# Attention's probabilities turned from streamed operand to weights in a one-core encoder block

## The chip, the core and the metric

The kernel runs on one core of a Trainium2 chip. A core has TensorE (PE; its weight loads are shown apart as PEld), VectorE (DVE), ScalarE (ACT), GpSimd (POOL) and a queue for transfers (SP). The metric is the device time of one execution in microseconds (us). The time given is the median of several runs; one more execution was taken by the profiler, and all rows of the trace come from that one.

## What is computed

One layer of an encoder block on 512 tokens of width 1024, in float32: a half step of a gated feed-forward net, then two token mixers side by side (an RWKV-7 recurrence and a "forgetting" attention, each 8 heads of 64), a gated sum of both, and a second half step. The change touches the attention:

```
def forgetting_attention(q, k, v, log_f):
    scale = 1.0 / np.sqrt(hd).astype(np.float32)
    cum = jnp.cumsum(log_f, axis=-1)
    ...
        s = jnp.einsum('bhqd,bhkd->bhqk', q_i, k, preferred_element_type=jnp.float32) * scale
        s = s + c_i[..., :, None] - cum[..., None, :]
        s = jnp.where(mask, s, -jnp.inf)
        pr = jax.nn.softmax(s, axis=-1)
        return jnp.einsum('bhqk,bhkd->bhqd', pr.astype(v.dtype), v)
```

The mask is causal, and the queries come in 4 blocks of 128. Query block b sees b + 1 blocks of 128 keys.

## The kernel before

Activations lie transposed, features on the partitions and the 512 tokens along the free dimension. Products that need near-float32 accuracy are made of three one-pass products of parts (`mm3`, L142). The attention's product with the values and the scan's small products take float32 operands as they are, and each such matmul shows as two instructions ("passes") in the trace, each with a weight load of its own.

The stage of the change runs two things at once and fills the rest. (a) The recurrence goes through 16 chunks of 32 tokens. Each chunk has three visits of TensorE with narrow weights of 32 or 64 columns: `product_x` (xps), `product_u` (ups) and `products_sy` (sps, yps). (b) The attention goes through four pairs of heads, and for each pair through three `Block`s: query blocks 0 and 1 together, then 2, then 3. (c) What is left of the input projection, columns pq and pgt of eight steps with three matmuls of 512 columns each, fills TensorE's time ("fills", rank FILL).

One `Block` (L1785) does this for its two heads q = 0, 1. `logits` (L1793): TensorE writes the logits of a head into a PSUM bank `lp` (tile pool pf, three banks). `maximum` (L1805): VectorE masks and takes the row extreme into `mx`. `exp` (L1813): ScalarE writes the exponentials to `pts` and their sum to `mx`. `divide` (L1817): VectorE takes the reciprocal of the sums and multiplies the probabilities by it, one instruction per query block and head. `turn` (L1824): TensorE transposes the probabilities, 128x128 at a time, back into `lp`. `copy_t` (L1828): ScalarE copies them to `tr`. `values` (L1832): the values `vt` are the weights (128 keys x 64), the transposed probabilities are streamed (128 queries), and the result stands transposed already, head q on partitions 64q to 64q + 63 of `lp[1]`. `copy_o` (L1841): VectorE copies it to its place in `qp`.

The order of the stage's instructions isn't left to the order of the code. `Plan` (L177) gets each step with an engine, an estimated duration, its dependencies, a rank (SCAN, SIDE, NEXT, ROWS, FILL) and the buffers that it takes and frees. `start` (L192) gives the earliest time that a step could begin, `run` (L208) makes the list by picking the step that begins first (the longer remaining way wins a tie), and writes the instructions in that order. `SWITCH` holds a price for each change between kinds of TensorE work ("w" 512-column products, "t" transposes, "m", "n" and "u" narrow ones). `Queued` (L60) holds VectorE, ScalarE and TensorE to the written order, and all their instructions of this stage then carry its line, L71. In `enter` (L1844) a block's steps are given to the plan. When the stage ends, the centering products `yc` (`first`, L1924) and the output projections `ppj` follow.

Of the kernel before, what the change touches and what calls it, by code (L numbers as in the profile page):

```python
# [9 lines left out]
F32 = mybir.dt.float32  # L10
# [3 lines left out]
ALU = mybir.AluOpType  # L14
# [4 lines left out]
P = 128  # L19
# [9 lines left out]
NB = T // P  # L29
# [21 lines left out]
def kernel(  # L51
# [24 lines left out]
    dve, act, pe = [Queued(e, False) for e in (nc.vector, nc.scalar, nc.tensor)]  # L76
# [97 lines left out]
    def on(do, *a):  # L174
        return lambda: do(*a)

    class Plan:  # L177
# [9 lines left out]
        def op(s, engine, us, do, *deps, rank=0, takes=(), frees=(), later=0.0, kind="w"):  # L187
            s.ops.append(dict(engine=engine, us=us, do=do, deps=deps, rank=rank, takes=takes, frees=frees, later=later,
                              kind=kind, end=None, way=0.0))
            return s.ops[-1]  # L190

        def start(s, o):  # L192
            to, now = o["engine"], s.idle.get(o["engine"], 0.0)
            ahead = 0.0 if to != "PE" else 0.57 if o["rank"] == SCAN else 0.26 if o["rank"] == SIDE and o["kind"] in "tw" else 0.31
            for d in o["deps"]:
                if d["end"] is None:
                    return None
                by = d["engine"]
                lag = 0.32 if by == "PE" else 0.15 if by == to else 0.21
                now = max(now, d["end"] + (0.0 if by == to == "PE" else lag + ahead))  # L200
            for name in set(o["takes"]):
                n = sum(t == name for t in o["takes"])
                if len(s.room[name]) < n:
                    return None
                now = max(now, sorted(s.room[name])[n - 1])
            return now

        def run(s):  # L208
            todo = list(s.ops)
            for o in s.ops[::-1]:  # L210
                o["way"] = o["way"] + o["us"] if o["rank"] != FILL else 0.0
                for d in o["deps"]:
                    d["way"] = max(d["way"], o["way"] + 0.3)
            while todo:
                at = {n: now for n, o in enumerate(todo) for now in [s.start(o)] if now is not None}

                def first(n):
                    o = todo[n]
                    turn = o["engine"] == "PE" and o["kind"] == "t" and s.kind in "mnu"
                    return at[n], -o["way"] - (40.0 if turn else 0.0), n  # L220

                n = min(at, key=first)
                o = todo[n]
                if o["engine"] in ("DVE", "ACT") and o["rank"] != SCAN:
                    until = at[n] + 0.98 * o["us"]
                    n = next((m for m in at if todo[m]["engine"] == o["engine"] and todo[m]["rank"] == SCAN
                              and at[m] < until), n)
                o = todo.pop(n)
                us = o["us"]
                if o["engine"] == "PE":  # L230
                    change = "".join("n" if k in "mnu" else k for k in (s.kind, o["kind"]))
                    us += s.SWITCH.get(change, 0.0) if s.kind != o["kind"] else 0.0
                    s.kind = o["kind"]
                s.idle[o["engine"]] = at[n] + us
                o["end"] = at[n] + us + o["later"]
                for name in o["takes"]:
                    s.room[name].remove(min(s.room[name]))
                for name in o["frees"]:
                    s.room[name].append(o["end"] + 0.33)
                if o["do"]:  # L240
                    o["do"]()

# [15 lines left out]
    class Norm:  # L258
# [7 lines left out]
        def scale(s, c, eng=None, src=None):  # L266
            g = pc(s.gain + c)
            src = xT[c][:] if src is None else src
            hi, lo = pair("h", c, s.place), pair("l", c, s.place)
            if eng is act:  # L270
                high = act.activation(hi[:], src, AF.Copy, scale=g)
            else:
                high = dve.tensor_scalar(hi[:], src, g, None, op0=ALU.mult)
            low = dve.scalar_tensor_tensor(lo[:], src, g, hi[:].bitcast(F32),
                                           op0=ALU.mult, op1=ALU.subtract)
            s.hi[c], s.lo[c] = hi, lo
            return high, low
# [813 lines left out]
    with ExitStack() as mx:  # L1091
# [302 lines left out]
        def half(q):  # L1394
            return slice(q * 64, (q + 1) * 64)

        class Rows(Columns):
# [26 lines left out]
            def sum(s, behind=None):  # L1424
                lo = s.part(1) if s.part else tmp("slo", dt=F32R)
                dve.tensor_tensor(lo[:], s.sq[:], f32(s.hi[:]), op=ALU.subtract)
                s.ps = bank("pq2", pf)
                with tc.issue_after(behind.ins) if behind else ExitStack():
                    for i, part in enumerate((s.hi, lo)):
                        last = pe.matmul(s.ps[:], bonesr[:], part[:], start=i == 0, stop=i == 1)  # L1430
                return last
# [18 lines left out]
        vt = []  # L1450
# [334 lines left out]
        class Block:  # L1785
# [13 lines left out]
                    pe.matmul(l, qb[q][:, bs], klc[q][:, 0:n], start=False, stop=True)  # L1799

            def of(s, q, b):
                mx = s.pair.mx[q]
                return slice(s.at[b], s.at[b] + (b + 1) * P), mx[:, b:b + 1], mx[:, NB + b:NB + b + 1]

            def maximum(s, q, b):  # L1805
                if s.pair.mx is None:
                    s.pair.mx = [tp.tile([P, 2 * NB], F32, tag=f"mx{i}", name=f"mx{i}", bufs=2) for i in range(2)]
                n, top, _ = s.of(q, b)
                l = s.lp[q][:, n]
                dve.tensor_tensor_reduce(l, l, dmask[:, T - (b + 1) * P:T], -1.0, 3e38, op0=ALU.add, op1=ALU.min,  # L1810
                                         accum_out=top)
# [2 lines left out]
                n, top, sum_ = s.of(q, b)  # L1814
                act.activation(pts[:, q, n], s.lp[q][:, n], AF.Exp, bias=top, scale=-1.0, accum_out=sum_)

            def divide(s, q):  # L1817
                sums = s.pair.mx[q][:, NB + s.bl[0]:NB + s.bl[-1] + 1]
                dve.reciprocal(sums, sums)
                for b in s.bl:  # L1820
                    n, _, sum_ = s.of(q, b)
                    dve.tensor_scalar(pts[:, q, n], pts[:, q, n], sum_, None, op0=ALU.mult)

            def turn(s, q):  # L1824
                for k in range(s.w // P):
# [5 lines left out]

            def values(s):  # L1832
                for j, b in enumerate(s.bl):
                    for k in range(b + 1):
                        o = s.at[b] + k * P
                        for q in range(2):
                            h = 2 * s.pair.p + q
                            pe.matmul(s.lp[1][half(q), j * P:(j + 1) * P], vt[k][:, h * 64:(h + 1) * 64],
                                      s.tr[q][:, o:o + P], start=k == 0, stop=k == b)

            def copy_o(s):  # L1841
                dve.tensor_copy(s.pair.qp[:, s.bl[0] * P:(s.bl[-1] + 1) * P], s.lp[1][:, 0:len(s.bl) * P])

            def enter(s, operands):  # L1844
                for q in range(2):
                    us = sum(0.455 * (b + 1) * P / T + 0.02 for b in s.bl)
                    sees.append(op("PE", us, on(s.logits, q), *operands[q], rank=SIDE, takes=["pf"]))
                lit = sees[-2:]
                for q in range(2):
                    o = []  # L1850
                    for b in s.bl:
                        n = (b + 1) * P
                        e = op("DVE", 0.18 + 1.05e-3 * n, on(s.maximum, q, b), lit[q], rank=SIDE)
                        o.append(op("ACT", 0.26 + 0.83e-3 * n, on(s.exp, q, b), e, *turned[q][-1:], rank=SIDE))
                    exps.extend(o)
                    us = 0.16 + sum(0.13 + 0.69e-3 * (b + 1) * P for b in s.bl)
                    o = op("DVE", us, on(s.divide, q), *o, rank=SIDE)
                    lit[q] = op("PE", 0.11 * s.w / P, on(s.turn, q), o, rank=SIDE, kind="t")
                for q in range(2):
                    turned[q].append(lit[q])  # L1860
                o = [op("ACT", 0.1 + 0.75e-3 * s.w, on(s.copy_t, q), lit[q], *copies[-1:], rank=SIDE, takes=["tr"],
                        frees=["pf"] * (1 - q)) for q in range(2)]
                copies.append(o[1])
                us = 0.22 * sum(b + 1 for b in s.bl)
                o = op("PE", us, s.values, *o, rank=SIDE, frees=["tr"] * 2, kind="n")
                return op("DVE", 0.13 + 0.55e-3 * len(s.bl) * P, s.copy_o, o, rank=SIDE, frees=["pf"])

        outs = []
        for p in range(NP):
# [314 lines left out]
```

## Time and profile before

| what | value |
|---|---|
| median of 3 runs | 1098.98 us (1097.88 to 1099.1) |
| the profiled execution | 1097.66 us |
| span of its instructions | 1095.8 us |
| clock granted to TensorE, mean | 0.998 |
| the 80 transposes of probabilities (lp<-ident,pts), busy | 13.0 us |
| the 160 passes of the values (lp<-tr,vt), busy | 11.4 us |

In the rows of a group stand the engine, the operation, what is written and read (for a matmul the streamed operand first, then the weights), the weights' rows*columns and the streamed shape, the count, the busy time, the mean duration of one in ns, and the idle time of the engine ahead of them. In the rows of a timeline stand the start and the duration in us; neighbours of one kind are merged into one row with their count. A matmul's duration holds its way through the array, so successive matmuls overlap, and the distance of their starts tells what one costs.

### The profile page before, as it was taken

To read this page: it belongs to the slowest core of one execution; us is meant where nothing else is said; L and a number is where in the kernel's file an instruction comes from. 1 tells how busy PE (TensorE), PEld (TensorE's weight loads), DVE (VectorE), ACT (ScalarE), POOL (GpSimd) and SP (SyncE) were. 2 spreads that over 40 slices of the span, in tenths; PEclk is the share of its full clock that TensorE was granted. 3 is DMA by queue.
4 is the path that set the end of the run, shared out by engine and by line. 5 is a ranking of instruction groups with operands and counts; after the bars stand their busy time and mean duration, and the time that the engine had idled before them with its cause. 6 is when DMAs were issued, how large, how long until landed. Compare 5 with 4: busy or idle time off the path is not lost.

```text
span 1095.8 us, 16697 instructions
## 1 busy us (share of the span) xinstructions
PE 1087.1 (99%) x6306; PEld 887.4 (81%) x6306; DVE 837.8 (76%) x1162; ACT 670.1 (61%) x1050; POOL 212.5 (19%) x255
## 2 busy tenths in 40 slices
PE   9999999999999999999999999999999999999997
PEld 7888888888887888888777777888888888888886
DVE  7997676789756699788877766877697766689874
ACT  6765556575554755346988856534576565576554
POOL 1211220134204112401000030112311202114210
PEclk9999999999999999999999999999999999999999
DMA  7989887879936434444112252645968888859972
GB/s 225 250 174 235 198 178 202 192 143 191 231 98 184 114 94 128 114 136 116 50 41 84 81 200 88 189 118 172 271 153 192 189 215 174 184 158 203 236 187 77
DMA packets 139725, 177.11 MB, mean 162 GB/s; under 512 B 9726, under 2 KB 75838, under 8 KB 139646
## 3 DMA queue, kind: packets, MB, share of 16 engines
q0 software_dynamic: 33328, 70.40, 33.7%
q1 hardware_dynamic: 105582, 104.21, 31.1%
q10 hardware_dynamic: 736, 1.45, 0.3%
q8 instruction: 50, 0.82, 0.3%
q14 instruction: 29, 0.24, 0.1%
HBM read 163.51 MB, written 12.52 MB: 161 GB/s over the span
## 4 chain that ended last, share of the span: by engine, by line
PE 97%; ACT 2%; DVE 1%; issue 0%; DVEq 0%; ACTq 0%
PE P L71 39%; PE P L145 5%; PE P L144 5%; PE P L143 5%; PE pgt L71 5%; PE lp L71 3%; PE pq L71 2%; PE ppj L71 2%; PE pk L145 2%; PE pk L143 2%; PE pk L144 2%; PE pb L71 2%; PE pa L71 1%; PE pw L144 1%; PE pw L145 1%; PE pw L143 1%
## 5 line engine op out<-in xcount | busy, mean ns | idle before, releaser
L71 PE MATMUL P<-sraw,q 128*128 128x512 f32 x344 | 91.3, 389 | 0.0
L135 ACT CAST whi<-raw 128x1024 fp32r<-128x1024 f32 (+3 forms) x43 | 41.1, 956 | 65.8 <-issue 19.3
L71 PEld LDWEIGHTS P<-sraw,q 128*128 128x128 f32 x344 | 64.6, 188 | 13.4
L71 PE MATMUL P<-swhi,q 128*128 128x512 f32 x224 | 71.4, 390 | 0.0
L71 PE MATMUL P<-sraw,wxh 128*128 128x512 f32 x200 | 68.4, 394 | 0.0
L136 DVE TENSOR_TENSOR wlo<-raw,whi 128x1024 fp32r<-128x1024 f32 (+3 forms) x44 | 49.6, 1127 | 16.3 <-ACT whi L135 15.2
L71 PE MATMUL P<-swhi,wxh 128*128 128x512 f32 x144 | 56.9, 395 | 0.0
L71 PE MATMUL P<-swhi,wxl 128*128 128x512 f32 x144 | 56.1, 390 | 0.0
L71 PE MATMUL P<-swlo,wxh 128*128 128x512 f32 x144 | 56.1, 389 | 0.0
L704 POOL DMA_DIRECT2D cb<-in_ffn_w_dram x20 | 24.1, 1204 | 150.1 <-DVE cd L71 85.3
L71 PE MATMUL P<-sraw,wxl 128*128 128x512 f32 x136 | 53.0, 390 | 0.0
L704 POOL DMA_DIRECT2D cd<-in_ffn_w_dram x24 | 29.5, 1229 | 102.6 <-DVE swlo L71 38.7
L71 PEld LDWEIGHTS P<-swhi,q 128*128 128x128 f32 x224 | 42.0, 188 | 8.7
L71 PE MATMUL P<-swlo,q 128*128 128x512 f32 x112 | 43.6, 389 | 0.0
L71 PEld LDWEIGHTS P<-sraw,wxh 128*128 128x128 f32 x200 | 37.2, 188 | 7.3
L71 ACT CAST sraw<-cd 128x1024 fp32r<-128x1024 f32 x30 | 31.5, 1050 | 15.1 <-PE P L71 11.5
L71 DVE TENSOR_TENSOR swlo<-ca,swhi 128x1024 fp32r<-128x1024 f32 x24 | 29.2, 1222 | 14.0 <-ACT swhi L71 14.0
L71 DVE TENSOR_TENSOR swlo<-cc,swhi 128x1024 fp32r<-128x1024 f32 x20 | 24.5, 1224 | 19.0 <-ACT swhi L71 18.7
L71 DVE TENSOR_TENSOR u<-P,u 128x512 f32<-128x512 f32 x52 | 34.1, 684 | 5.8 <-ACT u L71 5.7
L563 POOL DMA_DIRECT2D ca<-in_ffn_w_dram x16 | 19.3, 1205 | 96.2 <-DVE swlo L71 66.4
L143 PE MATMUL pk<-xh,whi 128*128 128x512 f32 x96 | 37.8, 394 | 0.0
L145 PE MATMUL pk<-xh,wlo 128*128 128x512 f32 x96 | 37.5, 391 | 0.2 <-DVE wlo L136 0.2
(616 smaller groups left out, 3446.9 us busy)
## 6 DMA issues: line engine op xcount, KB each, us to landing
raw<-in_w_in_dram SPq DMA_DIRECT2D x40, 512.0 KB
cc<-in_ffn_w_dram SPq DMA_DIRECT2D x36, 512.0 KB
cb<-in_ffn_w_dram POOLq DMA_DIRECT2D x36, 512.0 KB, 6.1
cb<-in_ffn_w_dram SPq DMA_DIRECT2D x32, 512.0 KB
cd<-in_ffn_w_dram POOLq DMA_DIRECT2D x32, 512.0 KB, 7.5
ca<-in_ffn_w_dram POOLq DMA_DIRECT2D x32, 512.0 KB, 7.6
ca<-in_ffn_w_dram SPq DMA_DIRECT2D x20, 512.0 KB
cd<-in_ffn_w_dram SPq DMA_DIRECT2D x18, 512.0 KB
```

Source lines behind the costliest of these rows:

```text
L71: q.last = do(*a, **kw)
L135: (hi_eng or act).copy(hi[:], raw[:])
L136: (eng or dve).tensor_tensor(lo[:], raw[:], hi[:].bitcast(F32), op=ALU.subtract)
L143: pe.matmul(ps, whi, xhi, start=first, stop=False, skip_group_check=onto)
L144: pe.matmul(ps, whi, xlo, start=False, stop=False, skip_group_check=onto)
L145: return pe.matmul(ps, wlo, xhi, start=False, stop=last, skip_group_check=onto)
L563: nc.gpsimd.dma_start(s.sum[g], src, accum_op=ALU.add)
L704: nc.gpsimd.dma_start(to, s.block(b, n, h), accum_op=ALU.add)
```

## The change

The values' product is turned round. The transposed probabilities become the weights (128 keys x 128 queries) and the values are streamed (64 columns), so the result stands with the queries on the partitions and the two heads side by side, 64 columns each. The probabilities are no longer divided: `divide` takes the reciprocals of the sums of both heads in one instruction (`mx` is now one tile for both), and `scale` multiplies the result by them as it reads it from PSUM, one instruction for a block. `turn_o` then transposes the result on TensorE, 128x128 for each query block, into another part of the same bank, and `copy_o` copies from there. So `turn` no longer waits for `divide`; `turn_o` waits for `scale`.

The plan's constants for delays, ties and switches are others, the values now count as kind "t", and the estimate of the values' duration stays 0.22 us for two heads and one block of keys. The list of the whole stage is made anew with them. Nothing outside the stage is edited, and no transfer is added or removed.

```
@@ -191,12 +191,13 @@
 
         def start(s, o):
             to, now = o["engine"], s.idle.get(o["engine"], 0.0)
-            ahead = 0.0 if to != "PE" else 0.57 if o["rank"] == SCAN else 0.26 if o["rank"] == SIDE and o["kind"] in "tw" else 0.31
+            ahead = 0.0 if to != "PE" else 0.74 if o["rank"] == SCAN else 0.29 if o["rank"] == SIDE else 0.3
+            ahead += 0.0 if o["kind"] == "m" != s.kind and o["rank"] != SCAN else 0.0
             for d in o["deps"]:
                 if d["end"] is None:
                     return None
                 by = d["engine"]
-                lag = 0.32 if by == "PE" else 0.15 if by == to else 0.21
+                lag = 0.37 if by == "PE" else 0.15 if by == to else 0.13
                 now = max(now, d["end"] + (0.0 if by == to == "PE" else lag + ahead))
             for name in set(o["takes"]):
                 n = sum(t == name for t in o["takes"])
@@ -216,19 +217,20 @@
 
                 def first(n):
                     o = todo[n]
-                    turn = o["engine"] == "PE" and o["kind"] == "t" and s.kind in "mnu"
-                    return at[n], -o["way"] - (40.0 if turn else 0.0), n
+                    turn = o["engine"] == "PE" and o["kind"] == "t" and s.kind in "mu"
+                    same = o["kind"] == s.kind == "m"
+                    return at[n], -o["way"] - (30.0 if turn else 200.0 if same else 0.0), n
 
                 n = min(at, key=first)
                 o = todo[n]
                 if o["engine"] in ("DVE", "ACT") and o["rank"] != SCAN:
-                    until = at[n] + 0.98 * o["us"]
+                    until = at[n] + 0.93 * o["us"]
                     n = next((m for m in at if todo[m]["engine"] == o["engine"] and todo[m]["rank"] == SCAN
                               and at[m] < until), n)
                 o = todo.pop(n)
                 us = o["us"]
                 if o["engine"] == "PE":
-                    change = "".join("n" if k in "mnu" else k for k in (s.kind, o["kind"]))
+                    change = "".join("n" if k in "mu" else k for k in (s.kind, o["kind"]))
                     us += s.SWITCH.get(change, 0.0) if s.kind != o["kind"] else 0.0
                     s.kind = o["kind"]
                 s.idle[o["engine"]] = at[n] + us
@@ -236,7 +238,7 @@
                 for name in o["takes"]:
                     s.room[name].remove(min(s.room[name]))
                 for name in o["frees"]:
-                    s.room[name].append(o["end"] + 0.33)
+                    s.room[name].append(o["end"] + 0.31)
                 if o["do"]:
                     o["do"]()
 
@@ -1799,12 +1801,12 @@
                     pe.matmul(l, qb[q][:, bs], klc[q][:, 0:n], start=False, stop=True)
 
             def of(s, q, b):
-                mx = s.pair.mx[q]
-                return slice(s.at[b], s.at[b] + (b + 1) * P), mx[:, b:b + 1], mx[:, NB + b:NB + b + 1]
+                mx = s.pair.mx
+                return slice(s.at[b], s.at[b] + (b + 1) * P), mx[:, 0, b, q:q + 1], mx[:, 1, b, q:q + 1]
 
             def maximum(s, q, b):
                 if s.pair.mx is None:
-                    s.pair.mx = [tp.tile([P, 2 * NB], F32, tag=f"mx{i}", name=f"mx{i}", bufs=2) for i in range(2)]
+                    s.pair.mx = tp.tile([P, 2, NB, 2], F32, tag="mx0", name="mx0", bufs=2)
                 n, top, _ = s.of(q, b)
                 l = s.lp[q][:, n]
                 dve.tensor_tensor_reduce(l, l, dmask[:, T - (b + 1) * P:T], -1.0, 3e38, op0=ALU.add, op1=ALU.min,
@@ -1814,12 +1816,9 @@
                 n, top, sum_ = s.of(q, b)
                 act.activation(pts[:, q, n], s.lp[q][:, n], AF.Exp, bias=top, scale=-1.0, accum_out=sum_)
 
-            def divide(s, q):
-                sums = s.pair.mx[q][:, NB + s.bl[0]:NB + s.bl[-1] + 1]
-                dve.reciprocal(sums, sums)
-                for b in s.bl:
-                    n, _, sum_ = s.of(q, b)
-                    dve.tensor_scalar(pts[:, q, n], pts[:, q, n], sum_, None, op0=ALU.mult)
+            def divide(s):
+                s.sums = s.pair.mx[:, 1, s.bl[0]:s.bl[-1] + 1, :].rearrange("p b q -> p (b q)")
+                dve.reciprocal(s.sums, s.sums)
 
             def turn(s, q):
                 for k in range(s.w // P):
@@ -1831,15 +1830,27 @@
 
             def values(s):
                 for j, b in enumerate(s.bl):
-                    for k in range(b + 1):
-                        o = s.at[b] + k * P
-                        for q in range(2):
-                            h = 2 * s.pair.p + q
-                            pe.matmul(s.lp[1][half(q), j * P:(j + 1) * P], vt[k][:, h * 64:(h + 1) * 64],
-                                      s.tr[q][:, o:o + P], start=k == 0, stop=k == b)
+                    for q in range(2):
+                        h = 2 * s.pair.p + q
+                        for k in range(b + 1):
+                            o = s.at[b] + k * P
+                            pe.matmul(s.lp[1][:, j * P + q * 64:j * P + q * 64 + 64], s.tr[q][:, o:o + P],
+                                      vt[k][:, h * 64:(h + 1) * 64], start=k == 0, stop=k == b)
+
+            def scale(s):
+                n = 2 * len(s.bl)
+                s.o = s.pair.qp[:, s.bl[0] * P:(s.bl[-1] + 1) * P]
+                dve.tensor_tensor(s.o.rearrange("p (b v) -> p b v", v=64),
+                                  s.lp[1][:, 0:n * 64].rearrange("p (b v) -> p b v", v=64),
+                                  s.sums.unsqueeze(2).broadcast_to([P, n, 64]), op=ALU.mult)
+
+            def turn_o(s):
+                for j in range(len(s.bl)):
+                    pe.transpose(s.lp[1][:, (2 + j) * P:(3 + j) * P], s.o[:, j * P:(j + 1) * P], ident[:])
 
             def copy_o(s):
-                dve.tensor_copy(s.pair.qp[:, s.bl[0] * P:(s.bl[-1] + 1) * P], s.lp[1][:, 0:len(s.bl) * P])
+                n = len(s.bl) * P
+                dve.tensor_copy(s.o, s.lp[1][:, 2 * P:2 * P + n])
 
             def enter(s, operands):
                 for q in range(2):
@@ -1853,17 +1864,18 @@
                         e = op("DVE", 0.18 + 1.05e-3 * n, on(s.maximum, q, b), lit[q], rank=SIDE)
                         o.append(op("ACT", 0.26 + 0.83e-3 * n, on(s.exp, q, b), e, *turned[q][-1:], rank=SIDE))
                     exps.extend(o)
-                    us = 0.16 + sum(0.13 + 0.69e-3 * (b + 1) * P for b in s.bl)
-                    o = op("DVE", us, on(s.divide, q), *o, rank=SIDE)
-                    lit[q] = op("PE", 0.11 * s.w / P, on(s.turn, q), o, rank=SIDE, kind="t")
+                    lit[q] = op("PE", 0.11 * s.w / P, on(s.turn, q), *o, rank=SIDE, kind="t")
                 for q in range(2):
                     turned[q].append(lit[q])
                 o = [op("ACT", 0.1 + 0.75e-3 * s.w, on(s.copy_t, q), lit[q], *copies[-1:], rank=SIDE, takes=["tr"],
                         frees=["pf"] * (1 - q)) for q in range(2)]
                 copies.append(o[1])
-                us = 0.22 * sum(b + 1 for b in s.bl)
-                o = op("PE", us, s.values, *o, rank=SIDE, frees=["tr"] * 2, kind="n")
-                return op("DVE", 0.13 + 0.55e-3 * len(s.bl) * P, s.copy_o, o, rank=SIDE, frees=["pf"])
+                divided = op("DVE", 0.2, s.divide, *exps[-2 * len(s.bl):], rank=SIDE)
+                o = op("PE", 0.22 * sum(b + 1 for b in s.bl), s.values, *o, rank=SIDE, frees=["tr"] * 2, kind="t")
+                n = len(s.bl)
+                o = op("DVE", 0.15 + 0.12 * n, s.scale, o, divided, rank=SIDE)
+                o = op("PE", 0.11 * n, s.turn_o, o, rank=SIDE, kind="t")
+                return op("DVE", 0.1 + 0.1 * n, s.copy_o, o, rank=SIDE, frees=["pf"])
 
         outs = []
         for p in range(NP):
```

## The prediction

> **What bounds the kernel now.** I read the page's busy times first, then its chain, then the busy times of the stage that holds the attention, then TensorE's own order of work there.
>
> ```profile
> span 1095.8 us, 16697 instructions
> PE 1087.1 (99%) x6306; PEld 887.4 (81%) x6306; DVE 837.8 (76%) x1162; ACT 670.1 (61%) x1050; POOL 212.5 (19%) x255
> PEclk9999999999999999999999999999999999999999
> PE 97%; ACT 2%; DVE 1%; issue 0%; DVEq 0%; ACTq 0%
> ```
> ```profile
> 515.00:649.00 134.00, 133.44 (x1766) 100.49 (x1766) 102.18 (x257) 110.57 (x291) 9.78 (x18) 1.00 0.27 79
> 649.00:663.00 14.00, 14.00 (x65) 11.64 (x63) 2.61 (x3) 5.28 (x7) 3.20 (x7) 1.00 0.73 232
> ```
>
> The second fence gives, for a stretch, its length and then the busy time of PE, PEld, DVE, ACT and POOL, the clock and the DMA. Attention and scan lie in 515 to 649 us. TensorE is idle there for 134.00 - 133.44 = 0.56 us. In the 14 us after it no attention and no scan matmul runs: they are columns of the input projection ("fills", pq and pgt), which the list puts wherever TensorE would otherwise wait. So a us of TensorE work added here is a us of the kernel; a us taken from VectorE or ScalarE is worth part of 0.56 us at most. A busy PE row overstates, since its ends are modelled; from here on I go by the starts.
>
> ```profile
> 643.73 0.40 PE L71 MATMUL pgt<-xl,whi 128*128 128x512 f32 x1
> 643.96 0.39 PE L71 MATMUL pgt<-xh,wlo 128*128 128x512 f32 x1
> 644.28 1.09 PE L71 MATMUL lp<-tr,vt 128*64 128x128 f32 x16
> 645.31 0.50 PE L71 MATMUL pgt<-xh,whi 128*128 128x512 f32 x1
> 645.64 0.40 PE L71 MATMUL pgt<-xl,whi 128*128 128x512 f32 x1
> ```
> ```profile
> 534.96 0.88 PE L71 MATMUL lp<-tr,vt 128*64 128x128 f32 x12
> 535.77 0.46 PE L71 MATMUL ups<-Xs,Tall 64*64 64x64 f32 x8
> ```
>
> The rows lp<-tr,vt are the products with the values that the change turns round: weights of 128x64, 128 columns streamed, two instructions (passes) for each f32 matmul, 160 in all (10 block sums x 4 pairs x 2 heads x 2 passes). They stand in 12 groups, the first at 534.96, the last at 644.28: eight of 12 passes, four of 16. From start to the next start a group of 12 takes 0.81 us, one of 16 takes 1.03. Four passes more cost 0.22, so a pass is 0.055 us, and a group has 0.81 - 12 x 0.055 = 0.15 us of its own for getting in and out.
>
> Around it is more. Fill follows fill after 0.23 us (643.73 to 643.96). The fill ahead of the group holds TensorE for 0.32 (+0.09), the first behind it for 0.33 and the second for 0.24 or so (together +0.11). So a group of this shape between fills costs 0.35 us beyond its passes.
>
> **The change part by part.**
>
> (1) *Probabilities as weights.* Still 160 passes, now with weights 128x128 and 64 columns streamed. No row has that shape, so two limits are taken from neighbours: the stream and the weight load.
>
> ```profile
> 663.47 2.74 PE L71 MATMUL yc<-V,center 128*128 128x512 f32 x6
> 665.64 0.79 PE L71 MATMUL ppj<-yh,whi 128*128 128x512 f32 x1
> ```
> ```profile
> L71 PEld LDWEIGHTS lp<-tr,vt 128*64 128x64 f32 x160 | 8.5, 136 | 3.0 <-issue 1.7 <-ACT BK L71 1.0
> L71 PEld LDWEIGHTS sps<-RD,RD 128*32 128x32 f32 x480 | 7.4, 109 | 4.8 <-issue 1.4 <-ACT qa L71 0.9 <-ACT pts L71 0.5
> L71 PEld LDWEIGHTS lp<-klc,qb 128*128 128x128 f32 x32 | 6.1, 190 | 0.4
> L71 PEld LDWEIGHTS yc<-V,center 128*128 128x128 f32 x6 | 1.1, 189 | 1.0 <-issue 0.5 <-PE pgt L71 0.2 <-PE yc L71 0.2
> ```
> ```profile
> 523.44 0.19 PEld L71 LDWEIGHTS lp<-kb,qa 128*128 128x128 f32 x1
> 523.56 0.19 PEld L71 LDWEIGHTS lp<-klc,qb 128*128 128x128 f32 x1
> 523.67 0.19 PEld L71 LDWEIGHTS lp<-kb,qa 128*128 128x128 f32 x1
> 523.78 0.19 PEld L71 LDWEIGHTS lp<-klc,qb 128*128 128x128 f32 x1
> 523.90 0.19 PEld L71 LDWEIGHTS lp<-kb,qa 128*128 128x128 f32 x1
> 524.02 0.19 PEld L71 LDWEIGHTS lp<-klc,qb 128*128 128x128 f32 x1
> ```
>
> Stream: yc is a full f32 product on 128x128 weights, six passes of 512 columns. Their starts go over into the next row after 2.17 us; the last pass overlaps it, so five take about 2.14, 0.43 us each. For 64 columns that is 0.43/8 = 0.054 us, which is what a pass takes now.
>
> Load: the column behind the bar gives the mean ns of a weight load. From 32 to 64 columns it grows by 27 ns, from 64 to 128 by 53: 0.83 ns a column, so 128 columns hold the load path for about 0.106 us. The third fence shows loads that have little to hide behind: the logits stream 128 or 256 columns to each, and the loads start every 0.11 to 0.12 us whatever is streamed (523.44 to 524.02: 0.58 for five). With 64 columns streamed, a load has 0.054 us of stream to lie under, and it needs 0.11.
>
> I take 0.11 us a pass, the nearest row (same weights, short stream). Below stands 0.054 (loads wholly hidden), above 0.054 + 0.106 = 0.16 (load and stream one after the other). The sum: 160 x 0.11 = 17.6 against 160 x 0.055 = 8.8, **+8.8 us**; ends -0.2 and +16.8.
>
> The Trainium skill, "TensorE: Matmul & The Clock Gate", section "LDWEIGHTS (loading the stationary operand)", states that a load takes the number of its columns divided by 1.2 ns, however many rows it has; its section on weight-path modes excludes float32 from the fast load. The trace agrees (0.83 ns a column). An estimate by that page alone is 160 x 107 ns = 17.1 us, half a us under mine. It speaks against the change: the columns moved from the stream to the load.
>
> (2) *Fewer switches of shape.* Passes over the full array enter and leave without the extra time: in the yc fence the next product starts 0.03 us behind the last pass. Of the 12 groups, six have full-array work on both sides (two of them a fill behind, four a transpose, which loses about 0.05 instead of 0.11):
>
> ```profile
> 641.34 0.44 PE L71 MATMUL xps<-RD,G 128*32 128x64 f32 x16
> 641.72 0.66 PE L71 MATMUL lp<-ident,pts 128*128 128x128 f32 x4
> 642.13 0.48 PE L71 MATMUL pgt<-xh,whi 128*128 128x512 f32 x1
> ```
> ```profile
> 648.74 0.60 PE L71 MATMUL yt<-ident,BK 128*128 128x128 f32 x4
> 649.10 0.48 PE L71 MATMUL pgt<-xh,whi 128*128 128x512 f32 x1
> 649.42 0.39 PE L71 MATMUL pgt<-xl,whi 128*128 128x512 f32 x1
> ```
>
> (four transposes behind a narrow group 0.41, behind a fill 0.36). Six x (0.15 + 0.09) + 2 x 0.11 + 4 x 0.05 = 1.9 us go. Five are followed by a narrow scan group, which still has to be entered: 5 x 0.15 = 0.75. One comes behind a scan group: about 0.2. Together **-2.8 us** if the neighbours stay alike. The list is made anew, so this may be 0 to -4.
>
> (3) *Transposing the result.* turn_o adds 4 per pair, 16 transposes, all full-array. From 648.74 to 649.42 lie four and one fill of 0.23: 0.45/4 = 0.11 each. **+1.8 us**.
>
> (4) *VectorE.*
>
> ```profile
> L71 DVE TENSOR_SCALAR pts<-pts,mx 128x512 f32<-128x512 f32 x8 | 3.9, 487 | 0.3
> L71 DVE TENSOR_SCALAR pts<-pts,mx 128x384 f32<-128x384 f32 x8 | 3.4, 421 | 0.4
> L71 DVE TENSOR_SCALAR pts<-pts,mx 128x256 f32<-128x256 f32 x8 | 2.8, 348 | 0.0
> L71 DVE TENSOR_SCALAR pts<-pts,mx 128x128 f32<-128x128 f32 x8 | 2.3, 287 | 0.3
> L71 DVE RECIPROCAL mx<-mx 128x1 f32<-128x1 f32 x16 | 2.6, 160 | 2.3 <-ACT pts L71 2.1
> L71 DVE COPY qk<-lp 128x128 f32<-128x128 f32 x8 | 2.3, 285 | 1.1 <-PE lp L71 1.1
> L71 DVE COPY qk<-lp 128x256 f32<-128x256 f32 x4 | 1.7, 423 | 1.0 <-PE lp L71 0.9
> ```
>
> The four scalings of the probabilities go (12.4 us) and half of the 24 reciprocals (12 x 0.16 = 1.9). Scaling the result comes: 12 reads of PSUM of the copy's sizes, 8 x 0.29 + 4 x 0.42 = 4.0. That frees some 10 us of VectorE, all beside a TensorE that is busy: 0 taken, -0.56 at most (the idle time above).
>
> (5) *New wait.* turn_o stands in TensorE's written order behind values, scale and VectorE's queue; fills are listed between. What is behind a late turn_o on TensorE waits too, a scan product among it. The nearest row is a logit that waited for a copy:
>
> ```profile
> 534.42 0.44 PE L71 MATMUL lp<-kb,qa 128*128 128x384 f32 x1 [0.27 <-ACT tr L71]
> ```
>
> 0 to 12 x 0.27 = 3.2 us; I take 0, as only 0.56 us of such idle time exists now. The plan still books 0.22 us for two heads' product, where I get 0.44; VectorE and ScalarE then find TensorE later than planned, which costs TensorE nothing.
>
> (6) *Banks and chain.* lp is held longer: values 0.7 to 0.9 more, scale 0.3 to 0.4, transposes 0.1 to 0.2, two handovers; a reciprocal and a scaling (0.5 to 0.7) go. Call it +0.7 to +1.3 a block, 8 to 16 us over 12 blocks if they follow one another closely. Cover: the 14 us of bare fills. Taken at 0.
>
> Sum: 8.8 - 2.8 + 1.8 = **+7.8 us**. The profiled execution took 1097.66 us, 1.86 outside its span of 1095.8; it would take 1105.5. The median of the runs, 1098.98, lies 1.32 above it: **1106.8 us**, 0.7% slower. Its own range is 1103.5 to 1110 (switches 0 to -4, waits 0 to 3.2).
>
> **Rivals.**
>
> *Loads hidden, stream decides* (0.054 a pass): -0.2 - 2.8 + 1.8 = -1.2, 1097.8. For it: other narrow groups load in parallel; against it the fence of the logits' loads. Chance 0.08.
>
> *Faster.* If a pass streamed at the rate of a fill, 0.23/8 = 0.028 us for 64 columns, with the load hidden: 160 x 0.028 = 4.5, so -4.3 - 2.8 + 1.8 = -5.3, 1093.7. Place: the 160 passes. It decides below (8.8 + 2.8 - 1.8 - 2.2)/160 = 0.048 us a pass. Against it: the yc rows stream f32 at half a fill's rate, and the loads. Chance 0.03, and 0.01 for an order that gains as much. The Trainium skill, "TensorE: Matmul & The Clock Gate", section "Back-to-back issue gap", has a table in which 1 to 64 columns take about 25 ns; by it this rival would be the forecast. Both rows named speak against its use here.
>
> *Load and stream one after the other* (0.16): +16.8 - 2.8 + 1.8 = +15.8, 1114.8. Logits with 256 columns (0.11 of stream) do not show it. Chance 0.06.
>
> *The attention outlasts the fills*: the chain of (6) uses up the 14 us and TensorE waits 2 to 5 us: 1109 to 1112. It needs the upper end of (6). Chance 0.10.
>
> **Numbers.** Forecast 0.72, the rivals 0.08, 0.04, 0.06 and 0.10. The range 1101 to 1112 leaves out the hidden loads, the faster case and the serial one, 0.18. What a measurement of this kernel tells from no change is about 0.2%, 2.2 us: faster 0.04, same 0.08, slower 0.88.
>
> **What would show it.** In the changed kernel's profile, lp rows with vt streamed against tr: weights 128x128, mean load 188 to 190 ns, starts 0.11 us apart (12 passes in 1.3 us, 16 in 1.75), the fill behind at 0.23. Sixteen transposes more at 0.11. Idle TensorE in the stage of 1 us or less, and at least some us of bare fills behind it. Starts 0.055 apart would make the forecast wrong; so would idle stretches of TensorE ahead of transposes of qk, or narrow groups that no longer stand where they stood.

## The result, and the profile after

| | before | after |
|---|---|---|
| median of the runs | 1098.74 us (1097.88 to 1099.1, 6 runs) | 1104.63 us (1104.55 to 1104.79, 6 runs) |
| profiled execution | 1097.66 us | 1104.56 us |
| span of its instructions | 1095.8 us | 1102.6 us |

The changed kernel is slower: ratio 1.0057, 95% interval 1.0047 to 1.0067, 5.9 us by the medians. The two profiled executions differ by 6.8 us in span; that of before lies 1.1 us under its median, that of after at its median. So the trace below has to account for 6.8 us, of which 0.9 is the place of one execution among its like.

The page of after, the busy times and the chain; then the stage and what follows it (length, then busy PE, PEld, DVE, ACT, POOL, clock, DMA):

```profile
span 1102.6 us, 16706 instructions
PE 1094.5 (99%) x6322; PEld 898.0 (81%) x6322; DVE 828.6 (75%) x1130; ACT 670.7 (61%) x1050; POOL 212.1 (19%) x255
PE 98%; DVE 1%; ACT 0%; DMA 0%; issue 0%; DVEq 0%; ACTq 0%
```
```profile
515.00:649.00 134.00, 134.00 (x1657) 105.77 (x1656) 85.90 (x207) 104.96 (x275) 7.57 (x14) 1.00 0.26 73
649.00:670.00 21.00, 21.00 (x192) 16.97 (x191) 10.02 (x21) 11.52 (x24) 4.80 (x9) 1.00 0.56 189
```

TensorE is idle for none of the 134 us, and VectorE has 16 us less to do in them; over the whole program it has 9.2 us less (837.8 before, 828.6 after), since part of its work now stands behind 649. The kernel lost time although VectorE got work taken off and ScalarE and GpSimd kept theirs within 0.6 us. What TensorE does instead stands in its own order, here a group of 16 passes between fills, and the load's row with its mean ns:

```profile
630.04 0.39 PE L71 MATMUL pgt<-xl,whi 128*128 128x512 f32 x1
630.27 0.40 PE L71 MATMUL pgt<-xh,wlo 128*128 128x512 f32 x1
630.50 1.90 PE L71 MATMUL lp<-vt,tr 128*128 128x64 f32 x16
632.21 0.48 PE L71 MATMUL pgt<-xh,whi 128*128 128x512 f32 x1
632.52 0.39 PE L71 MATMUL pgt<-xl,whi 128*128 128x512 f32 x1
```
```profile
L71 PEld LDWEIGHTS lp<-vt,tr 128*128 128x128 f32 x160 | 19.2, 191 | 0.9
```

The group takes 1.71 us from start to start, where one of 16 took 1.03. The fill ahead of it is no longer held up (630.27 to 630.50 is 0.23; it was 0.32). The fill behind it still holds TensorE longer than other fills, for 0.31 (it was 0.33). The load has the 190 ns that loads of 128 columns for products have in the rows of before.

To sum it up I took, for every TensorE instruction from the stage's start to the first yc, the distance from its start to the next start, and added these by kind (us):

| kind, count before and after | before | after | difference |
|---|---|---|---|
| values, 160 passes | 10.55 | 17.70 | +7.15 |
| transposes of the result, 0 and 16 | 0 | 1.09 | +1.09 |
| transposes of probabilities, 80 | 8.58 | 7.94 | -0.64 |
| transposes vp and bp of the scan, 64 | 7.28 | 6.48 | -0.80 |
| xps, 256 | 6.33 | 5.99 | -0.34 |
| fills, 354 | 89.69 | 90.12 | +0.43 |
| all else | 36.26 | 36.16 | -0.10 |
| sum | 158.69 | 165.48 | +6.79 |

Every us of the span's difference lies in this stage, and the values' passes alone make more than all of it.

### The profile page after: what moved, and what is told of

The parts are those of the page before. It is cut to its first block, busy times and chain, and to the rows that moved or that the text cites. A ratio compares the mean times of both kernels' runs of the same rounds, so it can differ in the third digit from the quotient of the medians.

```text
span 1102.6 us, 16706 instructions
## 1 busy us (share of the span) xinstructions
PE 1094.5 (99%) x6322; PEld 898.0 (81%) x6322; DVE 828.6 (75%) x1130; ACT 670.7 (61%) x1050; POOL 212.1 (19%) x255
## 3 DMA queue, kind: packets, MB, share of 16 engines
q10 hardware_dynamic: 736, 1.45, 0.3%
## 4 chain that ended last, share of the span: by engine, by line
PE 98%; DVE 1%; ACT 0%; DMA 0%; issue 0%; DVEq 0%; ACTq 0%
PE P L71 39%; PE P L144 5%; PE P L145 5%; PE P L143 5%; PE pgt L71 5%; PE lp L71 4%; PE pq L71 3%; PE ppj L71 2%; PE pk L145 2%; PE pk L143 2%; PE pk L144 2%; PE pb L71 1%; PE pa L71 1%; PE pw L144 1%; PE pw L145 1%; PE pw L143 1%
```

## The experiments

The theory: a pass on 128-column weights costs what the load of 128 columns costs, 0.11 us, twice the old pass; VectorE's relief and the order of the list are worth little. The rivals: the stream or a fixed price sets the pace; the turning round itself (scale, transpose, waits) costs; or the new list hides a larger price. Ratios are against runs of before on the same chip, whose medians lie between 1097.9 and 1098.3. The changed kernel's 1104.63 was measured beside a median of 1098.74, so a difference from it is uncertain by up to 0.8 us. Where a reading hangs on less, the sum over the stage, made from the trace as in the table above (158.69 before, 165.48 after), is given too; it can be compared between all versions.

**Twice the stream.**

```
-pe.matmul(s.lp[1][:, j * P + q * 64:j * P + q * 64 + 64], s.tr[q][:, o:o + P],
-          vt[k][:, h * 64:(h + 1) * 64], start=k == 0, stop=k == b)
+pe.matmul(s.lp[1][:, (2 * j + q) * P:(2 * j + q + 1) * P], s.tr[q][:, o:o + P],
+          vt[k][:, h * 64:(h + 1) * 64].unsqueeze(1).broadcast_to([P, 2, 64]), ...)
```

> The changed kernel, with each of the 160 passes streaming its 64 columns of values twice (128 columns; the second copy is not read). Nothing else is altered, the list is the same. Theory (the weight load of 128 columns sets the pace, 0.11 us a pass, and the stream lies under it): 64 columns at 0.43 us for 512 are 0.054 us, 128 are 0.107, still no more than the load, so a pass stays at 0.11 us and the time at 1104.6 us, within 1 us. Rival (the stream lies beside the load only in part, or sets the pace with something added): 160 x 0.054 = 8.6 us more, 1113.

(Beside this, `scale` reads the first 64 of each 128 columns.) Measured: 1105.12 us, ratio 1.006 (1.0045 to 1.0075), 0.5 us over the changed kernel; the sum over the stage is 165.68, 0.2 more. Its timeline:

```profile
631.11 1.95 PE L71 MATMUL lp<-vt,tr 128*128 128x128 f32 x16
632.81 0.48 PE L71 MATMUL pgt<-xh,whi 128*128 128x512 f32 x1
```

16 passes with 128 columns streamed take 1.70 us, with 64 they took 1.71. Within a group the passes of both versions start 0.111 to 0.112 us apart. The stream is covered; its second half came free but for the 0.2. The rival that put load and stream one after the other falls, too: it would have cost 8.6 us.

**Fewer weight columns.**

```
-pe.matmul(s.lp[1][:, j * P + q * 64:j * P + q * 64 + 64], s.tr[q][:, o:o + P],
+pe.matmul(s.lp[1][0:96, j * P + q * 64:j * P + q * 64 + 64], s.tr[q][:, o:o + 96],
```

> The changed kernel with weights of 96 columns instead of 128 in the values' passes: the last 32 queries of each block of 128 are left out of the product (their rows of the result are not computed). Stream, count of passes and list are the same. Theory (load sets the pace, 0.83 ns a column): 32 columns less are 0.027 us a pass, 160 x 0.027 = 4.2 us less: 0.085 us a pass, 1100.4 us. Rival (a fixed price of about 0.11 us for each full-array float32 pass, whatever its columns): no change, 1104.6.

Measured: 1100.44 us, ratio 1.002 (1.0011 to 1.003), 4.2 us under the changed kernel, as the theory had it; the sum over the stage is 161.36, 4.1 less, all of it in the values' passes. Its group and its load:

```profile
627.85 1.49 PE L71 MATMUL lp<-vt,tr 128*96 128x64 f32 x16
629.15 0.47 PE L71 MATMUL pgt<-xh,whi 128*128 128x512 f32 x1
```
```profile
L71 PEld LDWEIGHTS lp<-vt,tr 128*96 128x96 f32 x160 | 14.9, 164 | 1.0
```

1.30 us for 16, 0.081 each, and 0.085 from start to start within the group; the load lost 27 ns of its 191 and the pass lost as much (0.112 to 0.085). A fixed price for each pass is out. Anything else that would grow with the weight columns is not told apart from the load.

**Wide weights without turning round.** The values stay the weights, but those of both heads of the pair at once; each head uses its half.

```
-pe.matmul(s.lp[1][half(q), j * P:(j + 1) * P], vt[k][:, h * 64:(h + 1) * 64],
+pe.matmul(s.lp[1][:, (2 * q + j) * P:(2 * q + j + 1) * P], vt[k][:, 2 * s.pair.p * 64:(2 * s.pair.p + 2) * 64],
           s.tr[q][:, o:o + P], start=k == 0, stop=k == b)
```

> The kernel before, its product not turned round: values as weights, probabilities streamed, division on VectorE, the same list. Only the weights are made 128 columns wide: the values of both heads of the pair, of which the product of a head uses its own half; each head's result gets columns of its own and is copied by two instructions of 64 partitions. Theory (the number of weight columns sets the price): 160 passes at 0.112 us are 17.9 us where before has 10.55, less 1 us for switches of shape ahead of and behind the groups: 6.3 us over before, 1104.6, plus or minus 1. Rival (turning round, its scaling, transposing and waits cost, not the columns): 1098.3, within 1.

Measured: 1104.53 us, ratio 1.006 (1.0045 to 1.0076). This is the changed kernel's time with no scale, no transpose of the result and the old list. Its group between fills:

```profile
650.18 0.40 PE L71 MATMUL pgt<-xh,wlo 128*128 128x512 f32 x1
650.41 1.95 PE L71 MATMUL lp<-tr,vt 128*128 128x128 f32 x16
652.12 0.48 PE L71 MATMUL pgt<-xh,whi 128*128 128x512 f32 x1
652.44 0.39 PE L71 MATMUL pgt<-xl,whi 128*128 128x512 f32 x1
```

0.107 a pass from its row, and the same entry without extra time as after the change. Added up as above, the values cost 18.17 us here, 7.62 more than before, and everything else in the stage 1.0 less (147.15 against 148.14). TensorE's order is the same as in before, so the steps can be compared one by one: those next to the 12 groups are 1.3 us shorter, others 0.3 longer. So the price comes with the wide weights, and not with the direction of the product, the scaling or the new list. Taken alone this version doesn't tell the load from the stream: its passes load 128 columns and stream 128, on the whole array, and a pass can no longer run beside the other head's. The two versions above do that.

**No transposes of the result.**

```
-o = op("PE", 0.11 * n, s.turn_o, o, rank=SIDE, kind="t")
-dve.tensor_copy(s.o, s.lp[1][:, 2 * P:2 * P + n])
+dve.tensor_copy(s.o, s.lp[1][:, 0:n])
```

> The changed kernel without the 16 transposes of the result: the step is left out of the plan, and the copy takes the result as it lies, not transposed. The list is made anew without the step. Theory (a full-array transpose costs TensorE its own 0.07 to 0.11 us and its wait is hidden by fills): 1.1 to 1.8 us less, 1102.8 to 1103.5. Rival (the chain values, scale, transpose, copy makes TensorE wait): 3 us or more less, under 1101.6.

Measured: 1103.06 us, ratio 1.0042 (1.0025 to 1.0059), 1.6 us less; the sum over the stage is 163.83, 1.65 less. That is the step's own work and no wait worth naming: the transposes' own starts make 1.09 of it in the table, and the fills cost 0.36 less. The rest is within what a new list moves (below).

**Division kept on VectorE.** The reciprocals and scalings of the probabilities as before the change (`divide` itself is not shown below), `scale` only a copy:

```
-dve.tensor_tensor(s.o.rearrange(...), s.lp[1][:, 0:n * 64].rearrange(...), s.sums.unsqueeze(2).broadcast_to([P, n, 64]), op=ALU.mult)
+dve.tensor_copy(s.o, s.lp[1][:, 0:n * 64])
-lit[q] = op("PE", 0.11 * s.w / P, on(s.turn, q), *o, rank=SIDE, kind="t")
+o = op("DVE", us, on(s.divide, q), *o, rank=SIDE)
+lit[q] = op("PE", 0.11 * s.w / P, on(s.turn, q), o, rank=SIDE, kind="t")
```

> The changed kernel, but the probabilities are divided on VectorE ahead of their transposes as before the change (32 more scalings, 12 more reciprocals, some 14 us of VectorE), and the result is only copied from PSUM where it was scaled. Products and transposes are as in the changed kernel; the list is made anew. Theory (VectorE's relief is hidden behind TensorE): within 0.7 us of 1104.6. Rival (the relief of VectorE or the shorter chain took off several us, so that the turned product cost more than it shows): 1107 or more.

Measured: 1106.74 us, ratio 1.0075 (1.006 to 1.009), 2.1 us over the changed kernel; the sum over the stage is 167.20, 1.7 more. That missed: neither the 0.7 of the theory nor quite the rival's 2.4. The trace shows a late transpose that the changed kernel doesn't have, in the same place as in before; here in this version:

```profile
526.63 0.62 PE L71 MATMUL vp<-ident,V 128*64 128x128 f32 x4
527.54 0.66 PE L71 MATMUL bp<-ident,BK 128*128 128x128 f32 x4 [0.29 <-ACT BK L71]
528.13 0.45 PE L71 MATMUL xps<-RD,G 128*32 128x64 f32 x16
528.64 1.36 PE L71 MATMUL lp<-ident,pts 128*128 128x128 f32 x6
529.98 0.45 PE L71 MATMUL ups<-Xs,Tall 64*64 64x64 f32 x8
```

and in the changed kernel:

```profile
525.56 0.63 PE L71 MATMUL vp<-ident,V 128*64 128x128 f32 x4
525.95 0.31 PE L71 MATMUL lp<-kb,qa 128*128 128x128 f32 x1
```

Four vp take 0.91 us until bp may start, which waits for a copy on ScalarE (BK), where they take 0.39. ScalarE is what bp waits for there, not VectorE. But right behind it six transposes of probabilities take 1.34 us from start to the next start, where the same six, between the same neighbours, take 0.81 in the version of before without the scalings (below), and in the trace four of the six are released by a scaling on VectorE: the division that here stands ahead of them again. So some 0.5 us are lost behind the copy and as much behind the division, though the rows show only 0.29 of it as idle time; the rest lies under the ends of the instructions ahead. The version has a new list and a longer chain as well as more VectorE work, so two more runs took VectorE's work alone, with the list kept.

**VectorE's work alone.** More of it in the changed kernel:

```
 dve.reciprocal(s.sums, s.sums)
+for _ in range(2 * sum(1 + b // 2 for b in s.bl)):
+    dve.tensor_scalar(onesr[:], ones, 1.0, None, op0=ALU.mult)
```

> The changed kernel with 48 more VectorE instructions, four to eight behind each block's reciprocals, each multiplying a constant tile of 128 columns by one (nobody in the stage waits for them; by the 128-column scalings of before, 0.29 us each, 13.8 us in all). The list is the same. Theory (VectorE's relief is worth nothing to TensorE, and what the version with the division kept lost was due to its list and its longer chain): within 0.6 us of 1104.6. Rival (TensorE waits for a VectorE that is busier by 12 us): 2 us more, 1106.7.

Measured: 1104.32 us, ratio 1.0059 (1.0044 to 1.0074), no change against 1104.63 (sum over the stage 165.57, 0.1 more). There are four instructions behind each block's reciprocals. They brought less than the 13.8 us expected: VectorE has 9.0 us more in all (837.6 against 828.6), which is as much as the change had taken off it (9.2). Its stage, where VectorE now has 94.15 us instead of 85.90 and TensorE still no idle time:

```profile
515.00:649.00 134.00, 134.00 (x1657) 105.65 (x1656) 94.15 (x252) 105.15 (x276) 7.57 (x14) 1.00 0.25 74
```

Less of it in before:

```
 dve.reciprocal(sums, sums)
-for b in s.bl:
-    n, _, sum_ = s.of(q, b)
-    dve.tensor_scalar(pts[:, q, n], pts[:, q, n], sum_, None, op0=ALU.mult)
```

> The kernel before without the 32 scalings of the probabilities (left out: the result is not divided), 12.4 us of VectorE less and a shorter step ahead of the transposes; the list is the same. Theory (TensorE's idle time and late starts in the list of before come from ScalarE's copies, not from the scalings): within 0.6 us of 1098.3. Rival (the scalings hold up scan products and transposes): 1.3 to 2 us less, 1096.3 to 1097.0.

Measured: 1098.43 us, ratio 1.0004 (0.9995 to 1.0014), sum over the stage 158.79 against 158.69: nothing.

```profile
515.00:649.00 134.00, 133.41 (x1764) 100.53 (x1764) 91.07 (x226) 110.72 (x291) 9.28 (x18) 1.00 0.26 78
```
```profile
528.29 0.87 PE L71 MATMUL lp<-ident,pts 128*128 128x128 f32 x6
529.10 0.45 PE L71 MATMUL ups<-Xs,Tall 64*64 64x64 f32 x8
```

VectorE is 11 us lighter (102.18 before) and TensorE's busy time hasn't moved (133.44 before). So VectorE's amount of work was worth nothing to TensorE, added or taken off. What the version with the division kept lost is put down, by exclusion, to its list and to the division's place ahead of the transposes: in that list it made TensorE late, in the list of before its removal gained nothing. The rows above account for some 1.0 of the 1.7 us; how the rest divides between the two was not separated.

**The planner.** The changed code with the old planner, and the old code with the new one (the functions `start` and `run` exchanged as a whole):

> The changed kernel with the planner of before: its constants, ties and switch rule (the estimates of the steps stay those of the change). The list is made anew with them. Theory (the new constants moved only short waits of TensorE, 1 to 1.5 us in all): 1104.6 to 1106.1. Rival (the new list hides several us of the turned product's price): 1107.5 or more.

Measured: 1104.71 us, ratio 1.0061 (1.0047 to 1.0075), the changed kernel's time (sum over the stage 165.24, 0.2 less).

> The kernel before with the planner of the change: its constants, ties and switch rule, and nothing else. Theory: the list is worth 1.3 us either way, 1097.0 to 1099.6. Rival (the new list is the better one for any code, so that the turned product alone costs more than 6 us): 1096.3 or less.

Measured: 1099.38 us, ratio 1.0015 (1.0006 to 1.0023), 1.3 us slower than before on that chip (sum over the stage 160.33, 1.6 more). The new list does not suit the old code; its stage has idle time:

```profile
515.00:649.00 134.00, 131.86 (x1745) 99.59 (x1744) 101.96 (x257) 108.96 (x288) 7.56 (x14) 1.00 0.25 76
```

2.14 us idle where before has 0.56. The constants cost the old code 1.3 us and move the new one by 0.2 at most; they hide nothing of the price.

**An attempt at something better than before.** If a switch of shape costs, narrow groups should stand side by side:

```
+late = 1.0 if o["engine"] == "PE" and o["kind"] == "n" and s.kind not in "mu" else 0.0
-return at[n], -o["way"] - (40.0 if turn else 0.0), n
+return at[n] + late, -o["way"] - (40.0 if turn else 0.0), n
```

> The kernel before, with one rule added to its planner: the values' product is put back by up to 1 us while TensorE's last work was not a narrow scan product, so that it tends to stand right behind one and shares a switch of shape with it. Theory (a shared visit saves some 0.2 us, and six of the 12 groups stood between full-array work): 0.4 to 1.2 us under before, 1097.1 to 1097.9. Rival (the later product lengthens the chain of a block, and the list gets new waits): 1098.3 or more.

Measured: 1102.17 us, ratio 1.0038 (1.0025 to 1.005), 4.1 us slower than before on that chip (sum over the stage 161.53, 2.8 more). The rule did its part: 11 of the 12 groups stand right behind a scan product. Little was saved by it, since idle time alone grew by 3.0 us, and TensorE lost this to scan products that wait for ScalarE and VectorE:

```profile
515.00:645.00 130.00, 126.40 (x1723) 95.18 (x1722) 98.10 (x251) 106.22 (x284) 9.03 (x17) 1.00 0.25 77
```
```profile
L71 PE MATMUL sps<-RD,RD 128*32 128x64 f32 x480 | 9.8, 222 | 0.7 <-ACT RD L71 0.7
L71 PE MATMUL ups<-Xs,Tall 64*64 64x64 f32 x128 | 7.3, 230 | 1.0 <-DVE gs L71 1.0
L71 PE MATMUL yps<-RD,G 128*32 128x64 f32 x256 | 6.6, 220 | 1.2 <-ACT BK L71 1.2
```

3.6 us idle in 130. The "up to 1 us" of the expectation was wrong, too: the rule works on each choice anew, so the last group went behind all fills, from 644.28 to 665.46, and the first yc follows it at 666.48. No bare fills are left there; by the starts, another 0.7 us is lost behind the stage. None of the versions run here beats the kernel before.

## Why the prediction was right

The direction and the mechanism held, and 1104.63 lies in the range; the forecast of 1106.8 was 2.2 us too high. (The narrower range that the prediction calls its own, 1103.5 to 1110, does not come out of its terms: switches of 0 to -4 and waits of 0 to 3.2 give 1105.6 to 1112.8, and the measurement lies 1.0 under that.) By its steps:

(1) *Probabilities as weights*, forecast 0.11 us a pass, 17.6 in all: measured 17.70, 0.111 a pass. The two runs that altered the stream and the columns show that the weight columns set the pace, and the version with wide weights shows that the price comes without turning round. One sentence of this step went past a contradiction in its own rows. It gave 0.054 us for 64 streamed columns "which is what a pass takes now"; but the old pass streams 128, which by the yc rows should take 0.107, and took 0.055. The starts in the trace of before tell why: the passes of the two heads, which write to different halves, start 0.007 us apart, and the next two 0.109 after these. Two narrow passes run side by side. This left the sum right, since both numbers of the sum were measured or rightly bounded, but it is part of why the old form was cheap. The rule for loads of the Trainium skill ("TensorE: Matmul & The Clock Gate", section "LDWEIGHTS (loading the stationary operand)") gave 17.1 as an estimate, 0.6 under the measurement. The table in that page's section "Back-to-back issue gap" is given by the Trainium skill for isolated matmuls, with no weight load counted; so it was no forecast for these passes, which took 0.111 us.

(2) *Fewer switches*, forecast -2.8, of which 1.8 lie inside the groups. The values' net of +7.15 holds that part (8.8 - 1.8 = 7.0). The other us was to come from the neighbours. In the version that keeps the old list, everything but the values fell by 1.0, so the size holds, but in part by luck, since its pieces were others. The step ahead of a group became 0.09 shorter at 11 of the 12 groups (1.0 us), where the prediction counted six. A transpose behind became 0.06 shorter at four, as forecast, but a fill behind only 0.02 (0.32 for 0.34), where 0.11 had been taken. The sign "the fill behind at 0.23" failed: it is 0.31 to 0.32 here and in the changed kernel. The prediction had read it off the yc fence: the product there does start 0.03 us behind the last pass, but then holds TensorE for 0.63, so the rest of the pass's price had only moved into its step. It is the same with the values: a group of 16 takes 1.71 and the fill behind 0.08 more, together 16 x 0.112. In the changed kernel all else but values and transposes of the result fell by 1.45.

(3) *Transposing the result*, forecast 1.8. Their own starts make 1.09, but that is not all of their price. Many of the 16 are the last of their group, and the fill behind starts 0.03 to 0.09 us after them, for example

```profile
660.88 0.33 PE L71 MATMUL lp<-ident,qk 128*128 128x128 f32 x1
660.97 0.48 PE L71 MATMUL pgt<-xh,whi 128*128 128x512 f32 x1
661.28 0.39 PE L71 MATMUL pgt<-xl,whi 128*128 128x512 f32 x1
```

where part of the price is in the fill's longer step (0.31 instead of 0.23). My 0.11 had been taken with that step in it. Nine of the 16 have a fill or a logit with such a step behind them, 0.08 to 0.09 each, so with it the price comes to some 1.9 at most; part of that step may be there without them. The version without the transposes was 1.6 us faster. So the forecast size holds within 0.2 or so.

(4) *VectorE*, forecast 0: shown for the amount of its work by the two runs with the list kept. Its place ahead of the transposes is another matter, as the version with the division kept shows.

(5) *New wait*, forecast 0: TensorE has no idle time in the stage after the change.

(6) *Chain and cover*, forecast that 8 to 16 us of lengthening would stay under 14 us of bare fills. The last attention step on TensorE moved from 644.28 to 660.88, and bare fills from 662.79 to the first yc at 670.41 remain, 7.6 us where there were 14. The cover held, with about half left.

Terms and table together: forecast 8.8 - 2.8 + 1.8 = 7.8; measured 7.15 + 1.09 - 1.45 = 6.8 in span. The missing 1.0 us lies mostly in rows from which the prediction expected little: the transposes vp and bp and those of the probabilities cost 1.44 us less after the change, and the fills 0.43 more. Of the 1.44, some 0.5 is the late bp of before: four vp take 0.92 us there until bp may start, which waits for the copy on ScalarE. Another 0.15 are six transposes behind the division (0.96 us from 527.84, against 0.81 without the scalings). The rest was not separated from the order of the new list; taking the division out of the old list gained nothing. Of the other 1.2 us of the miss, 0.9 lie between the span's difference and that of the medians, since the profiled execution of before lies 1.1 us under its median, and the rest in the median of before, which moved from 1098.98 to 1098.74 with more runs.

## What to carry to other kernels

Before a product is turned round, count the weight columns that are loaded and the columns that are streamed, each with its duration from the trace. Here, with weights over the whole array, the longer of the two was the price of a matmul, and doubling the shorter one cost next to nothing; with narrow weights two passes ran side by side, and the sum had to be taken from the starts. Work taken off an engine that the bound engine does not wait for is worth nothing; here 11 us less of VectorE moved no time. Where such work stands, and whether the bound engine waits behind it, has to be read from the order, and a late start can hide under a row that looks busy. And a list that is made anew can move a kernel by a us or more (1.3 here with the planner's constants alone, 4.1 with one rule), so an edit that reorders has to be judged with the order held, where that can be done.

## What the runs showed of the hardware

A full-array float32 pass with 128 weight columns took 0.107 us in the mean of a group of 16 between fills, whether 64 or 128 columns were streamed (1.71 and 1.70 us for 16), and 0.111 to 0.112 from start to start within a group. With 96 weight columns it was 0.081 and 0.085.

Narrow float32 passes run side by side: with 64 weight columns, the passes of two heads on different halves of the array started 0.007 us apart and the next two 0.109 after these, 0.055 us a pass, where the yc rows put one stream of 128 columns at 0.107.

Full-array float32 passes follow a 512-column product without the extra 0.09 us that a 64-column group costs there. The 512-column product behind them still holds TensorE for 0.31 to 0.32 instead of 0.23, while their own last pass takes 0.03 to 0.09 instead of 0.112. In the version with wide weights and the old list the steps next to the 12 groups were 1.3 us shorter, and all steps but the values' 1.0.
